# A third PSUM bank in two stages, other gather paces, and part of a one-hot build moved from VectorE to ScalarE

## The chip, the core and the metric

The kernel runs on one core of a Trainium2 chip. A core has five engines with a queue each, and each works through its queue in order: PE (TensorE, the matrix products; PEld is its load of the stationary operand), DVE (VectorE), ACT (ScalarE), POOL (GpSimd, which issues the gathers here) and SP (SyncE, which issues most transfers). They meet through semaphores. Products land in PSUM, eight banks of 128 x 512 f32 numbers; another engine has to carry them out before a bank can be used again. The metric is the device time of one launch in microseconds (us).

## What is computed

One layer of a hybrid trunk over 1024 tokens of width 1024. An attention branch (MLA) and a gated linear attention branch (GLA) are mixed into h; then comes the part on which this change bears, a product-key mixture of 16384 experts, of which each of 8 heads picks 16 per token:

```python
def peer_ffn(h, w_q, sub_keys, u_tab, v_tab):
    q = (h @ w_q).reshape(B, L, PEER_HEADS, 2, PEER_HALF)
    s = jnp.einsum('blhpd,pnd->blhpn', q, sub_keys).astype(jnp.float32)
    top_s, top_i = lax.top_k(s, PEER_TOPK)
    ...
    idx = jnp.take_along_axis(cand_i..., best_pos, axis=-1)   # i * 128 + j
    gate = jax.nn.softmax(best_s, axis=-1)
    ...
        u = u_tab[ib]
        act = jax.nn.gelu(jnp.einsum('bpd,bphkd->bphk', hb, u).astype(jnp.float32), approximate=False)
        coef = (act * gb).astype(hb.dtype)
        return jnp.einsum('bphk,bphkd->bpd', coef, v_tab[ib])
```

## The kernel before

The 1024 tokens are eight blocks of 128, in two groups of four. Each group goes through `mla`, `mix` (GLA and the branch gates), `out_proj`, `norm_ffn` and `route` (the picks). The experts are then computed in two ways at once.

**Gathered.** For blocks 0 to 2 each picked row of u and v is fetched by an indirect transfer on POOL (`gather`, L115), and VectorE takes a dot product with it (L1361) or adds it, scaled, to `acc` (L1377): 448 dots (64 of them for the second half of block 3's tokens, whose results go into the gate values) and 384 adds. They come from one generator, `gather_all`; each call of `weights` takes `self.rate` steps of it. The rates are the constants R_... at the top, and R_VONLY and R_DENSE hold in the dense stage. At most six gathered rows are in flight.

**Dense.** For blocks 4 to 7 and half of block 3 (`DB`, 640 columns, of which 576 take part in the u products) all 16384 experts are computed. The experts are 128 groups `e` of 128: `u_stage(e)` multiplies one 128 x 1024 slice of u with the tokens (48 products of 128 x 288 in two halves, each in a PSUM bank with the tag `tr`) and ScalarE carries each half out with Gelu (L1466). `v_stage(q, half)` multiplies the coefficients of four groups with a half of v's columns (60 products of 128 x 512 in the five banks `mm`), and VectorE adds the five banks to `acc` (L1530). All products are in three parts (L86, L87, L88), since each f32 operand is split into a high part (ScalarE, L79) and a low part (VectorE, L80). So each weight slice costs a transfer of 512 KB (L908), a cast on ScalarE and a subtraction on VectorE. Tags hold two buffers in `tr` and `wr`/`wh`/`wl`, six in `at` and `cf`.

Between them stands the gate: `gate_matrix` turns the picks of the five blocks into a full table of gates per token and expert. Per block, the picks' i, j and gate values are transposed into `tt`. Then 16 rounds follow, each for eight tokens: `gh` holds for each token the 128 x 128 rows (iota == j) * gate (eight instructions, L1619), `oh` the rows (iota == i) for all eight (L1620), TensorE multiplies the two per token (eight products, 16 records, L1625), and ScalarE copies the result from two `mm` banks into `stage` (L1626), which is stored to DRAM (`d_gate`) after every fourth round. `oh` and `gh` are two buffers of the tag `cf`, so three rounds have buffers. 31 of the u stages are woven into these rounds (`weave`), five more must follow the last round (`NLATE`, a dependency on `gm_last`).

In `dense` the gates come back in quarters `q` into `gbuf`; `coef(q, j)` multiplies them with the activations (L1505, the first 576 columns), copies the last 64 columns (L1504) and splits the result into `cf` (L79, L80). Then v stages alternate with the remaining u stages.

The order of the instructions on each engine isn't the order of the code: a scheduler with a timeline of its own fixes it at build time, from the dependencies, the buffers and the code's order as priority. So a change of one buffer count moves instructions in all later stages.

## Time and profile before

| | us |
|---|---|
| three timed runs | 3827.49, 3832.95, 3835.60 (median 3832.95) |
| the profiled execution's own time | 3828.28 |
| its span in the trace | 3826.5 |
| PE busy | 3551.3 (93%) |
| DVE busy | 2999.0 (78%) |
| POOL busy | 1523.7 (40%) |
| ACT busy | 1320.1 (34%) |

The shares are means over stages with different limits. Along the span the stages are: first group up to about 1010 us, attention of the second group to 1250, its mix and projection to 1690, its route to 1950, the gate stage to 2326, v stages alone to about 2750, v and u stages in turn to 3795, and a tail of gathered adds. A matmul's record in the trace is longer than its share of the engine, since matmuls overlap: the distance from start to start tells what one costs. The granted clock (PEclk) is 1.00 at 2.4 GHz and 0.50 at 1.2 GHz.

### The profile page before, as it was taken

The numbers are of one execution on the slowest core, as the hardware profiler recorded it, in microseconds if no ns is written. First come the engines' busy times: TensorE is split into PE (matmuls) and PEld (weight loads), VectorE is DVE, ScalarE is ACT, GpSimd is POOL, SyncE is SP. The second block draws the span as 40 slices with busy tenths as digits, with TensorE's granted clock in tenths as the row PEclk, the third lists the DMA queues.
The fourth block names the chain that finished last, engine by engine and source line by source line (L and its number), as shares of the span: only waits on it lengthen the run. The fifth ranks groups of instructions, "written<-read, shape, count | busy, mean of one in ns | idle before, by whom it ended". The sixth has DMA issues, their size and how long they took to land.

```text
span 3826.5 us, 56688 instructions
## 1 busy us (share of the span) xinstructions
PE 3551.3 (93%) x20380; PEld 3088.1 (81%) x20385; DVE 2999.0 (78%) x6559; ACT 1320.1 (34%) x2851; POOL 1523.7 (40%) x1199
## 2 busy tenths in 40 slices
PE   8899998999799999899999998999999999999996
PEld 8787797777688788679898997777788888888885
DVE  5545444379877667559999997999988988898898
ACT  4656333232366334222244333222222222222221
POOL 2432333334332344322232223444455555555555
PEclk9999999999899999899999999999999999999998
DMA  4544634665324998665567879999999889999888
GB/s 160 173 159 141 222 131 130 192 212 186 124 69 114 341 353 299 268 225 203 171 227 275 288 280 372 332 342 344 332 334 338 303 315 325 322 348 322 298 324 318
DMA packets 390779, 976.98 MB, mean 255 GB/s; under 512 B 40464, under 2 KB 155664, under 8 KB 387680
## 3 DMA queue, kind: packets, MB, share of 16 engines
q1 hardware_dynamic: 242048, 508.50, 37.8%
q0 software_dynamic: 148448, 464.86, 34.6%
q8 instruction: 160, 2.62, 0.3%
q14 instruction: 123, 1.01, 0.1%
HBM read 825.61 MB, written 147.51 MB: 254 GB/s over the span
## 4 chain that ended last, share of the span: by engine, by line
PE 31%; DVE 24%; DMA 9%; issue 5%; ACT 1%; SPq 0%; POOL 0%; ACTq 0%; DVEq 0%; POOLq 0%
PE mm L86 6%; PE mm L87 6%; PE mm L88 6%; DVE cf L1619 4%; DVE acc L1377 3%; DVE row L1361 3%; DVE wl L80 3%; PE tr L88 3%; PE tr L86 3%; DMA wr<-in_uT 3%; PE tr L87 3%; DVE cf L1620 2%; DVE big L1530 2%; DMA row<-in_u,ids 2%; DMA row<-in_v,ids 1%
## 5 line engine op out<-in xcount | busy, mean ns | idle before, releaser
L115 POOL DMA_INDIRECT row<-in_v,ids x384 | 494.6, 1288 | 692.3 <-DVE acc L1377 274.1
L115 POOL DMA_INDIRECT row<-in_u,ids x384 | 479.5, 1249 | 590.8 <-issue 129.9
L86 PE MATMUL tr<-ar,wh 128*128 128x288 f32 x2048 | 616.9, 302 | 32.0 <-ACT at L1466 32.0
L79 ACT CAST wh<-wr 128x1024 fp32r<-128x1024 f32 x344 | 360.4, 1048 | 747.9 <-PE mm L88 302.8
L87 PE MATMUL tr<-ar,wh 128*128 128x288 f32 x2048 | 610.8, 299 | 0.0
L88 PE MATMUL tr<-ar,wl 128*128 128x288 f32 x2048 | 602.7, 301 | 8.5 <-DVE wl L80 8.1
L1361 DVE CUSTOM_DVE_ANT_0 row<-row,n2b 128x1024 f32<-128x1024 f32 x448 | 544.1, 1221 | 60.8 <-DMA row<-in_u,ids 51.0
L87 PE MATMUL mm<-wl,cf 128*128 128x512 f32 x1280 | 508.9, 398 | 5.1 <-DVE wl L80 5.0
L1377 DVE SCALAR_TENSOR_TENSOR acc<-row,act,acc 128x1024 f32<-128x1024 f32 x384 | 491.9, 1281 | 22.2 <-DMA row<-in_v,ids 20.0
L88 PE MATMUL mm<-wh,cf 128*128 128x512 f32 x1280 | 507.8, 397 | 0.0
L86 PE MATMUL mm<-wh,cf 128*128 128x512 f32 x1280 | 443.8, 398 | 15.0 <-DVE big L1530 8.6
L86 PEld LDWEIGHTS tr<-ar,wh 128*128 128x128 f32 x2048 | 392.4, 192 | 38.8 <-ACT at L1466 36.6
L80 DVE TENSOR_TENSOR wl<-wr,wh 128x1024 fp32r<-128x1024 f32 x264 | 324.6, 1229 | 103.2 <-ACT wh L79 98.9
L88 PEld LDWEIGHTS tr<-ar,wl 128*128 128x128 f32 x2048 | 387.5, 191 | 11.7 <-DVE wl L80 11.7
L87 PEld LDWEIGHTS tr<-ar,wh 128*128 128x128 f32 x2048 | 392.3, 192 | 2.1
L80 POOL TENSOR_TENSOR wl<-wr,wh 128x1024 fp32r<-128x1024 f32 x80 | 194.4, 2433 | 326.2 <-ACT wh L79 307.2
L86 PEld LDWEIGHTS mm<-wh,cf 128*128 128x128 f32 x1280 | 238.1, 188 | 80.5 <-ACT wh L79 9.9
L87 PEld LDWEIGHTS mm<-wl,cf 128*128 128x128 f32 x1280 | 241.9, 189 | 65.7 <-DVE wl L80 8.2
L88 PEld LDWEIGHTS mm<-wh,cf 128*128 128x128 f32 x1280 | 242.0, 189 | 58.8
L1530 DVE TENSOR_TENSOR big<-mm,big 128x512 f32<-128x512 f32 x320 | 204.4, 680 | 19.0 <-PE mm L88 18.9
L1466 ACT ACTIVATE at<-tr 128x288 f32<-128x288 f32 x212 | 87.0, 410 | 345.9 <-PE tr L88 326.1
L1625 PE MATMUL mm<-cf,cf 128*128 128x128 f32 x1280 | 158.4, 277 | 28.5 <-DVE cf L1620 28.5
(448 smaller groups left out, 7747.6 us busy)
## 6 DMA issues: line engine op xcount, KB each, us to landing
wr<-in_uT SPq DMA_DIRECT2D x128, 512.0 KB
wr<-in_vb SPq DMA_DIRECT2D x128, 512.0 KB
d_gate<-big SPq DMA_DIRECT2D x20, 2048.0 KB
big<-d_gate SPq DMA_DIRECT2D x128, 320.0 KB
d_wl<-wl SPq DMA_DIRECT2D x72, 512.0 KB
wl<-d_wl SPq DMA_DIRECT2D x72, 512.0 KB
at<-d_act SPq DMA_DIRECT2D x58, 288.0 KB
wr<-in_w_q SPq DMA_DIRECT2D x32, 512.0 KB
```

What stands on the lines that cost most here:

```text
L79: self.pace = self.nc.scalar.copy(hi, src)
L80: i = (eng or self.nc.vector).tensor_tensor(lo, src, hi.bitcast(F32), ALU.subtract)
L86: first = mm(ps, lh, rh, start=start, stop=False)
L87: mm(ps, lh, rl, start=False, stop=False)
L88: self.pe_last = mm(ps, ll, rh, start=False, stop=stop)
L115: i = self.nc.gpsimd.indirect_dma_start(out=out, out_offset=None, in_=self.a[table], in_offset=bass.IndirectOffsetOnAxis(ap=idx, axis=0))
L1361: lag(nc.vector.tensor_tensor_reduce(out=u, in0=u, in1=held[b][0], op0=ALU.mult, op1=ALU.add, scale=1.0, scalar=0.0, accum_out=act[:, 0, k ...
L1377: lag(nc.vector.scalar_tensor_tensor(acc, v, act[:, 1, k:k + 1], acc, ALU.mult, ALU.add))
L1466: self.nc.scalar.activation(at[:, ts], ps[:, :HD], AF.Gelu)
L1530: nc.vector.tensor_tensor(o, ps[b], o, ALU.add)
L1619: nc.vector.tensor_scalar(gh[:, k], self.iota, tt[:, 1, t + k:t + k + 1], tt[:, 2, t + k:t + k + 1], ALU.is_equal, ALU.mult)
L1625: self.gm_last = nc.tensor.matmul(ps[:, k], oh[:, kk], gh[:, kk], start=True, stop=True)
```

## The change

- `gpsum` (mix, route) and `dpsum` (gate stage, dense stage) give tiles without a count of their own three PSUM banks instead of two; with the five `mm` banks that makes eight. The tag `tr` is the one concerned; the three places that name its count say 3.
- R_VONLY goes from 2.5 to 2.6 and R_DENSE from 3.3 to 3.5.
- In `coef` the copy L1504 of the first quarter's coefficients (q = 0, four of 128) is VectorE's.
- In `gate_matrix`, for blocks 4 to 7 and every fourth round, ScalarE builds `gh`: Abs(iota - j), then Relu(gate - 2 * that), which is the gate where j matches and 0 elsewhere, since the gates of these blocks lie between 0 and 1. The negated j is made once per block (`nj`). That is 16 of the 80 rounds; the fifth block, number 3, is built as before.

```diff
@@ -58,7 +58,7 @@
 BANKS = [dict(zip(("S", "tr", "mm", "pv"), map(int, str(x)))) for x in (BA, BB)]
 NGA, NGR, F_MLA = 14, 14, 0.9
 RA0, NRU, NLATE = 7, 22, 5
-R_MLA, R_MIX, R_ROUTE, R_BUILD, R_VONLY, R_DENSE = 0.0, 2.8, 0.7, 2.4, 2.5, 3.3
+R_MLA, R_MIX, R_ROUTE, R_BUILD, R_VONLY, R_DENSE = 0.0, 2.8, 0.7, 2.4, 2.6, 3.5
 
 
 class Layer:
@@ -801,7 +801,7 @@
     def mix_pools(self, ctx):
         if self.grp == 0:
             self.g1 = self.pool(ctx, "yA")
-        self.psum = self.pool(ctx, "gpsum", 2, space=PSUM)
+        self.psum = self.pool(ctx, "gpsum", 3, space=PSUM)
         self.wk = self.pool(ctx, "gw", 2)
         if self.grp == 0:
             self.arp = self.pool(ctx, "arpA", 2)
@@ -959,7 +959,7 @@
             self.weave(self.gla_proj(g, h, st[h], nxt), inner, 1.8)
             self.run(inner)
             inner = self.gla_inner(g, h, st[h])
-        self.weave(self.raw_gates(g, range(first, 2 * NC), ("w_ob", 0), "tr", 2), inner, 1.0)
+        self.weave(self.raw_gates(g, range(first, 2 * NC), ("w_ob", 0), "tr", 3), inner, 1.0)
         self.run(inner)
         if g == 0 and NGF:
             self.fetch_n(self.nh, self.nl)
@@ -1466,7 +1466,7 @@
             self.nc.scalar.activation(at[:, ts], ps[:, :HD], AF.Gelu)
 
     def lead_gate(self, key, nxt):
-        self.run(self.raw_gate(1, self.gate_keys().index(key), nxt, "tr", 2))
+        self.run(self.raw_gate(1, self.gate_keys().index(key), nxt, "tr", 3))
 
     def lead_u(self, key, nxt):
         e = key[1]
@@ -1479,7 +1479,7 @@
     def dense(self, ctx):
 
         nc, a = self.nc, self.a
-        self.psum = self.pool(ctx, "dpsum", 2, space=PSUM)
+        self.psum = self.pool(ctx, "dpsum", 3, space=PSUM)
         self.wk = self.pool(ctx, "dw", 2)
         ng = NK // EG
         ndb = len(DB)
@@ -1501,7 +1501,7 @@
             at = acts.pop(q * EG + j)
             at3 = at.rearrange("p (b t) -> p b t", t=32)
             m = NU // 32
-            nc.scalar.copy(at3[:, m:], gbuf[:, q % 2, m:, j])
+            (nc.scalar.copy if q else nc.vector.tensor_copy)(at3[:, m:], gbuf[:, q % 2, m:, j])
             nc.vector.tensor_tensor(at3[:, :m], at3[:, :m], gbuf[:, q % 2, :m, j], ALU.mult)
             self.split(cf[:, 0], cf[:, 1], at)
 
@@ -1607,6 +1607,9 @@
             nc.tensor.transpose(pt[:, 2], pk["gate"].rearrange("p h k -> p (h k)"), self.ident)
             tt = self.t(self.wk, [P, ND], F32, "at", NAT)[:, 0:3 * P].rearrange("p (a t) -> p a t", a=3)
             nc.scalar.copy(tt, pt[:, 0:3])
+            if blk >= GB:
+                nj = self.t(self.sm, [P, P], F32, "nj128", 2)
+                nc.scalar.mul(nj, pt[:, 1], -1.0)
             yield
             for t32 in range(4):
                 if t32:
@@ -1615,7 +1618,14 @@
                     oh, gh = [self.t(self.wk, [P, 2 * ND], F32, "cf", NCF)[:, 0:NK * G8].rearrange("p (t j) -> p t j", j=NK) for _ in range(2)]
                     t = t32 * 32 + q * G8
                     tb = lambda i: tt[:, i, t:t + G8, None].broadcast_to([P, G8, NK])
-                    for k in range(G8):
+                    if blk >= GB and q == 3:
+
+                        for k in range(G8):
+                            nc.scalar.activation(gh[:, k], self.iota, AF.Abs, bias=nj[:, t + k:t + k + 1])
+                        for k in range(G8):
+                            nc.scalar.activation(gh[:, k], gh[:, k], AF.Relu, bias=tt[:, 2, t + k:t + k + 1], scale=-2.0)
+                    else:
+                      for k in range(G8):
                         nc.vector.tensor_scalar(gh[:, k], self.iota, tt[:, 1, t + k:t + k + 1], tt[:, 2, t + k:t + k + 1], ALU.is_equal, ALU.mult)
                     nc.vector.tensor_tensor(oh, iota, tb(0), ALU.is_equal)
                     for k4 in range(2):
```

The lines of `gate_matrix` move down by ten: L1619 is L1629 after the change, L1620 L1630, L1625 L1635 and L1626 L1636; the new ones are L1624 (Abs) and L1626 (Relu).

**PE at the end of the gate stage.** `tr` is a half of a u stage, `mm` a half round of the gate (two rows of x4 make a round). Before:

```order
L87 MATMUL tr_23306<-ar_16385,wh_23139 128x288
L88 MATMUL tr_23306<-ar_16384,wl_23140 128x288
L1625 MATMUL mm_23222<-cf_23212,cf_23211 128x128 x4
L1625 MATMUL mm_23228<-cf_23212,cf_23211 128x128 x4
L1625 MATMUL mm_23245<-cf_23235,cf_23234 128x128 x4
L1625 MATMUL mm_23251<-cf_23235,cf_23234 128x128 x4
L86 MATMUL tr_23356<-ar_16384,wh_23267 128x288
L87 MATMUL tr_23356<-ar_16385,wh_23267 128x288
```

After (20 rows of L1635 stand here one behind the other; ten are shown):

```order
L87 MATMUL tr_23442<-ar_16385,wh_23275 128x288
L88 MATMUL tr_23442<-ar_16384,wl_23276 128x288
L1635 MATMUL mm_22966<-cf_22956,cf_22955 128x128 x4
L1635 MATMUL mm_22972<-cf_22956,cf_22955 128x128 x4
L1635 MATMUL mm_22989<-cf_22979,cf_22978 128x128 x4
L1635 MATMUL mm_22995<-cf_22979,cf_22978 128x128 x4
L1635 MATMUL mm_23014<-cf_23004,cf_23003 128x128 x4
L1635 MATMUL mm_23089<-cf_23004,cf_23003 128x128 x4
L1635 MATMUL mm_23106<-cf_23096,cf_23095 128x128 x4
L1635 MATMUL mm_23112<-cf_23096,cf_23095 128x128 x4
L1635 MATMUL mm_23129<-cf_23119,cf_23118 128x128 x4
L1635 MATMUL mm_23135<-cf_23119,cf_23118 128x128 x4
```

Before, the u products reach to the last two rounds; after, all of those that may stand ahead of the last round do so ten rounds earlier, and the last ten rounds stand without any between them.

**ACT in a gate round.** After the change, in the first block, from the first copies on (`cf` is `gh`, `big` is `stage`, `at` with `tr` an evacuation of a u stage, `wh` the cast of a weight):

```order
L1636 COPY big_19326<-mm_19346 128x128x4
L1636 COPY big_19326<-mm_19352 128x128x4
L1624 ACTIVATE cf_19471<-iota,nj_3360_19333 128x128 x8
L1466 ACTIVATE at_19663<-tr_19679 128x288
L1626 ACTIVATE cf_19471<-cf_19471,at_19331 128x128 x4
L1636 COPY big_19326<-mm_19369 128x128x4
L1626 ACTIVATE cf_19471<-cf_19471,at_19331 128x128 x3
L1636 COPY big_19326<-mm_19375 128x128x4
L1626 ACTIVATE cf_19471<-cf_19471,at_19331 128x128
L1636 COPY big_19326<-mm_19392 128x128x4
L1636 COPY big_19326<-mm_19464 128x128x4
L79 CAST wh_19806<-wr_19804 128x1024
```

Eight Abs of a later round stand in one piece; the eight Relu are broken up by copies and an evacuation of a u stage, and the next weight's cast stands behind all of them.

**ACT between the gate stage and the first v stage.** `cf` from `at` is the cast of a coefficient, which waits for the gates. Before:

```order
L1466 ACTIVATE at_23495<-tr_23511 128x288
L1466 ACTIVATE at_23495<-tr_23537 128x288
L79 CAST wh_23574<-wr_23572 128x1024
L1504 COPY at_23333<-big_23259 128x64
L1504 COPY at_23409<-big_23259 128x64
L1504 COPY at_23488<-big_23259 128x64
L1504 COPY at_23564<-big_23259 128x64
L79 CAST cf_23335<-at_23333 128x640
L79 CAST cf_23411<-at_23409 128x640
L1466 ACTIVATE at_23571<-tr_23587 128x288
L79 CAST cf_23490<-at_23488 128x640
L1466 ACTIVATE at_23571<-tr_23613 128x288
```

After:

```order
L79 CAST wh_23713<-wr_23711 128x1024
L1466 ACTIVATE at_23631<-tr_23676 128x288
L79 CAST cf_23471<-at_23469 128x640
L79 CAST cf_23550<-at_23548 128x640
L79 CAST cf_23626<-at_23624 128x640
L1466 ACTIVATE at_23710<-tr_23726 128x288
L1466 ACTIVATE at_23710<-tr_23752 128x288
L1466 ACTIVATE at_23779<-tr_23800 128x288
L1504 COPY at_23853<-big_23395 128x64
L1504 COPY at_23855<-big_23395 128x64
L1466 ACTIVATE at_23779<-tr_23826 128x288
L79 CAST wh_23782<-wr_23780 128x1024
```

The four copies have left the queue, and three casts stand where the copies stood, ahead of the same four evacuations (two u stages).

## Rows read from the trace of the kernel before

**Rows 1.** Stretches: us, busy of PE, PEld, DVE, ACT, POOL, clock, DMA share, GB/s

```profile
1950.00:2326.00 376.00, 347.46 (x2761) 341.51 (x2761) 375.97 (x865) 147.70 (x259) 83.98 (x74) 1.00 0.78 278
2420.00:2750.00 330.00, 319.69 (x1349) 251.27 (x1348) 315.48 (x418) 85.11 (x135) 143.36 (x113) 1.00 0.95 340
2750.00:3795.00 1045.00, 1013.14 (x5698) 896.81 (x5696) 925.19 (x1182) 264.84 (x445) 588.49 (x453) 0.99 0.91 322
2361.50:2367.50 6.00, 5.94 (x25) 5.94 (x26) 2.02 (x2) 0.94 (x3) 0.94 (x1) 0.50 1.05 406
```

**Rows 2.** Groups from 1950 to 2326 us: busy, mean ns | idle before

```profile
L1619 DVE TENSOR_SCALAR cf<-iota,at 128x128 f32<-128x128 f32 x640 | 174.7, 352 | 0.0
L1625 PE MATMUL mm<-cf,cf 128*128 128x128 f32 x1280 | 158.4, 277 | 28.5 <-DVE cf L1620 28.5
...
L1377 DVE SCALAR_TENSOR_TENSOR acc<-row,act,acc 128x1024 f32<-128x1024 f32 x35 | 44.8, 1279 | 0.0
...
L80 DVE TENSOR_TENSOR wl<-wr,wh 128x1024 fp32r<-128x1024 f32 x30 | 36.5, 1217 | 0.0
```

**Rows 3.** VectorE in the gate stage in order of time: start, duration

```profile
2100.68 2.14 DVE L1619 TENSOR_SCALAR cf<-iota,at 128x128 f32<-128x128 f32 x8
2102.73 1.22 DVE L1620 TENSOR_TENSOR cf<-iota,at 128x1024 f32<-128x1024 f32 x1
2103.86 1.22 DVE L80 TENSOR_TENSOR wl<-wr,wh 128x1024 fp32r<-128x1024 f32 x1
2105.00 1.22 DVE L1361 CUSTOM_DVE_ANT_0 row<-row,n2b 128x1024 f32<-128x1024 f32 x1
2106.14 0.08 DVE L1361 DVE_READ_ACCUMULATOR2_ANT act<- 128x1 f32 x1
```

**Rows 4.** TensorE: two rows in order of time, then line L1625 (first, last start)

```profile
2104.09 2.02 PE L1625 MATMUL mm<-cf,cf 128*128 128x128 f32 x16 [0.61 <-DVE cf L1620]
2105.87 0.38 PE L88 MATMUL tr<-ar,wl 128*128 128x288 f32 x1
...
L1625 PE MATMUL mm<-cf,cf x1280: 270/275/377, 1955.8 to 2324.9; 128*128 128x128 f32 x183
```

**Rows 5.** TensorE around its stop, in order of time

```profile
2349.03 0.29 PE L86 MATMUL tr<-ar,wh 128*128 128x288 f32 x1
...
2350.49 0.29 PE L88 MATMUL tr<-ar,wl 128*128 128x288 f32 x1
2361.56 0.61 PE L86 MATMUL tr<-ar,wh 128*128 128x288 f32 x1 [10.78 <-ACT at L1466]
```

**Rows 6.** ScalarE groups of near shapes, whole span

```profile
L714 ACT ACTIVATE kjk<-qr 128x128 bf16<-128x128 f32 x64 | 19.8, 309 | 1.1
...
L785 ACT ACTIVATE pr<-S,snm 128x144 f32<-128x144 f32 x16 | 6.1, 383 | 2.8 <-DVE snm L783 2.8
```

**Rows 7.** ScalarE behind the gate stage, in order of time

```profile
2355.47 0.68 ACT L1504 COPY at<-big 128x64 f32<-128x64 f32 x4 [7.38 <-DMA big<-d_gate]
2356.31 1.39 ACT L79 CAST cf<-at 128x640 fp32r<-128x640 f32 x2 [0.16 <-ACT at L1504]
2361.10 0.41 ACT L1466 ACTIVATE at<-tr 128x288 f32<-128x288 f32 x1 [3.40 <-DMA d_act<-at]
2361.41 0.72 ACT L79 CAST cf<-at 128x640 fp32r<-128x640 f32 x1
```

**Rows 8.** VectorE in the tail: first and last row of the 17 adds

```profile
3794.54 5.23 DVE L1377 SCALAR_TENSOR_TENSOR acc<-row,act,acc 128x1024 f32<-128x1024 f32 x4
...
3819.56 2.61 DVE L1377 SCALAR_TENSOR_TENSOR acc<-row,act,acc 128x1024 f32<-128x1024 f32 x2 [0.68 <-DMA row<-in_v,ids]
```

**Rows 9.** TensorE's waits from 2420 to 3795 us: total, times, longest

```profile
PE tr L86 <- ACT at L1466: 21.2, 19, 3.8
```

**Rows 10.** ScalarE, then TensorE, around 2965 us, in order of time

```profile
2964.56 1.04 ACT L79 CAST wh<-wr 128x1024 fp32r<-128x1024 f32 x1 [14.47 <-DMA wr<-in_uT]
...
2965.97 0.61 PE L86 MATMUL tr<-ar,wh 128*128 128x288 f32 x1 [3.59 <-ACT at L1466]
```

## The prediction

> **What bounds the kernel now.** I read the stretches first, since the page's shares average over stages with different limits [rows 1]. In the gate stage (1950 to 2326 us) VectorE is busy 375.97 of 376 us, TensorE 347, ScalarE 148: VectorE is the bound there, and nowhere later so clearly. From 2420 to 2750 us (v stages alone) TensorE has 320 of 330 and VectorE 315: nearly level. From 2750 to 3795 us TensorE has 1013 of 1045 and VectorE 925: TensorE is the bound, beside DMA engines at 0.91. So a cut in VectorE's work is worth most in the gate stage, little in the next, nothing in the long last one. Then I read who waits in the gate stage [rows 2]: TensorE's one-hot matmuls (L1625) wait 28.5 us in all for VectorE, and the VectorE groups have no idle time before them.
>
> **The gate stage.** VectorE's prices are taken from start to start [rows 3]: eight gated rows of L1619 take 2102.73 - 2100.68 = 2.05 us (0.256 each), the one-hot of i (L1620) 1.13, a weight's low half (L80) 1.14, a dot product of a gathered row (L1361) 1.14. Busy means are 0.08 longer, as the 1.22 of L80 against 1.14; a gathered add (L1377) with a mean of 1.279 [rows 2] is then 1.20. The order before has, between the first and the last of the 80 rounds, 640 rows of L1619, 80 of L1620, 29 of L80, 35 dots and 35 adds: 163.8 + 90.4 + 33.1 + 39.9 + 42.0 = 369 us. That is the stage, so the prices hold. After, 16 rounds (every fourth of four of the five blocks) leave their 128 gated rows to ScalarE: minus 128 x 0.256 = 32.8 us. The order adds one L80 and two dots and drops an add in the stretch: 339 us. If VectorE stayed the bound all through, the stage would lose **30 us**.
>
> It doesn't stay so. On TensorE a round is 16 records, of which the next work starts 2105.87 - 2104.09 = 1.78 us later [rows 4], and a record of a u product (128x288) is (2350.49 - 2349.03) / 11 = 0.133 us [rows 5]. Before: 80 x 1.78 + 1427 x 0.133 = 332 us, well under VectorE's 369. After, 1173 u products stand ahead of the first round instead of 1117 (7 us more, of which some 2 fall into holes), and the order has moved u products ahead in the stage too: by round 65 TensorE has 65 x 1.78 + 1253 x 0.133 = 282 us to do, VectorE up to round 67, the most that six cf buffers (three rounds) let it be ahead, 408 x 0.256 + 67 x 1.13 + 58 x 1.14 + 28 x 1.20 = 280 us. So TensorE, now without its 28.5 us of waits, sets the pace up to there. Then the u products run out (the last ten rounds stand in one piece) and VectorE has 13 rounds left, all in the old form, the fifth block's: 104 x 0.256 + 13 x 1.13 + 9 x 1.14 + 6 x 1.20 = 59 us, which nothing covers. From first to last round: 5 + 282 + 59 = 346 against 369 (1955.8, the first round, to 2324.9 [rows 4]). That is 23; for late gated rows I take off 3: **-20 us**, with 10 and 30 as ends.
>
> ScalarE's side has no row of this form. Below is L714 with 0.309 us for 128x128 without a pointer operand, above L785, 0.383 for 128x144 out of PSUM with one [rows 6]. Successors overlap by some 0.05 to 0.1, as L79's 1.39 for two casts where one takes 0.72 [rows 7]. I take 0.30 per activation, nearer the upper row since both passes have a pointer as bias: 256 x 0.30 = 77 us on an engine with 376 - 148 = 228 free. No table load was added among them. ScalarE therefore has the time; what it can lose is the order, below.
>
> The Trainium skill (ScalarE: Activation LUTs, Rules for kernel authors) says to put relu and the like on VectorE and not on ScalarE, which speaks against this change. By its formula in the section on ACT_TABLE_LOAD (pointer bias 280 ns + 0.833 ns per element, less 93 of overlap) two passes cost an estimated 0.59 us for VectorE's 0.256, and counted as engine time the edit would lose 256 x 0.294 - 33 = 42 us. The stretch contradicts the use of that rule here, as VectorE is full and ScalarE 39% busy; no run here shows Abs or Relu yet.
>
> **From the last round to the first v product.** TensorE stops for 10.78 us at 2350.49 [rows 5]. ScalarE's queue explains it [rows 7]: the copies of L1504 wait for the gates to come back from DRAM until 2355.47, then casts, and the next evacuation (L1466) waits 3.40 us more for a d_act store that had to free its buffer. The two tr banks are full meanwhile. After it the granted clock is 0.50, the 1.2 GHz level [rows 1]: 25 records in 6 us, 0.24 apart instead of 0.133; over the 24 to 48 records of the spell that costs some 3 us. The q = 0 copies now go to VectorE, but the order shows that ScalarE gains nothing directly: three casts of cf, which need the same gates through VectorE, take the place of the copies ahead of the last four evacuations. What helps is the third tr bank: half a u product more (24 x 0.133 = 3.2 us) before the stop, and less clock lost. Against that TensorE comes out of ten thin rounds (1.78 us of work in some 4.5) and may start its u products at 1.2 GHz. Ends: 0 and 14; I take **-7 us**.
>
> **The pace.** R_VONLY from 2.5 to 2.6: in the 24 steps from the first to the twenty-fifth v stage the order has 130 gathered dots and adds instead of 124, 6 x 1.17 = 7 us of VectorE where it is nearly level with TensorE (15 us free [rows 1]). **+4 us**, ends 0 and 7. R_DENSE from 3.3 to 3.5: in the order each v stage with two u products holds 12 gathered operations before and after; something else holds the gathers there, so nothing changes. What comes of both is the tail: 17 adds stand behind the last L1530 before, 12 after. From 3794.54 to 3822.17 the 17 took 27.6 us, 1.63 each, a part of it waiting for rows [rows 8]; five fewer: **-8 us**, ends -5 and -10.
>
> **The third tr bank elsewhere.** From 2420 us TensorE waits 21.2 us in 19 pieces for ScalarE's evacuation [rows 9], so a third bank looks worth those 21 us and the clock lost after them. One level up it isn't so: at 2961 to 2966 ScalarE's weight cast (L79) had waited 14.47 us for the transfer from in_uT and ended at 2965.60; the evacuation behind it in the queue let TensorE go at 2965.97 [rows 10]. The next u product needs that very weight, so a free bank would have gained 0.37 us. I count 0, with -15 as end. In the mix stages no wait of the trace names a tr bank: 0, with 8 either way for the new order.
>
> **Sum.** -20 - 7 + 4 - 8 = -31 us. On the profiled execution's own 3828.28 that gives 3797; its span is 3826.5. The median of the three runs, 3832.95, is 4.7 higher and gives 3802. I take **3799 us**.
>
> **The rivals.** (1) VectorE stays the bound to the end, because TensorE finds holes for the moved u products: 30 instead of 20 in the stage, and the freed bank gives a little more: 3775 to 3787. For it: VectorE has no idle time at all in the stage. Against: the 59 us at its end. Chance 0.17. (2) ScalarE is late. In its queue the casts of weights and evacuations stand behind eight Abs or Relu; VectorE's L80 waits for the casts, TensorE for the rest. Half the stage's gain goes: 3812 to 3825. Against: three of five banks and buffers as cover. Chance 0.16. (3) The same mechanism beyond its cover makes it **slower**. A gated round's row buffer comes free three rounds ahead, 3 x 4.2 = 12.6 us; sixteen activations (4.8 us at 0.30) and what stands among them (148 / 80 = 1.85 us of other ScalarE work a round [rows 1], over two rounds some 4) take 9. Each us beyond 12.6 stops TensorE 16 times; the chain must reach 15 us, 0.69 us an activation, for the whole 31 and 8 more to go: 3841 to 3860. No row is near that price. Chance 0.07. (4) The change moves nothing that can be told: a new order in the mix stages or a later gate transfer takes the gain: 3825 to 3840. Chance 0.07.
>
> **How the numbers follow.** The forecast, 3787 to 3812, has what is left, 0.53. The range may leave out 0.2: (3), (4) and the upper third of (2): 3776 to 3820. A measurement of this kernel can tell some 0.2% from no change, 7.7 us. Faster by more: forecast, (1) and (2), 0.86; within it 0.07; slower 0.07.
>
> **What would show it.** Right: in the profile after, the last L1625 (now L1635) some 20 us earlier, its waits for VectorE gone from the first four blocks and present in the fifth; VectorE with idle time in the stage; Abs and Relu at 0.35 to 0.42 us each; 12 adds in a tail of some 20 us; the 3 to 4 us stops at weights from in_uT still there. Wrong: TensorE's waits for L1626 (Relu), L80 waiting for ScalarE's casts in the gate stage, or a gate transfer that lands as late as before.

## The result and the profile after the change

The changed kernel takes **3795.97 us** (median of six runs, 3791.68 to 3801.69) beside 3829.69 before (six runs, 3824.69 to 3835.60): ratio **0.9931**, 95% interval 0.9916 to 0.9946. (Ratios and intervals are the recorded ones throughout; the quotient of the two medians alone is 0.9912, so a step of 0.002 between two ratios should not be leaned on.) The profiled run has a span of 3794.4 us, 32.1 less than before. The forecast was 3799 within 3776 to 3820.

Where the 32 us come from is read by cutting both traces at the same instructions. The marks: the first instruction of L1050 (mix of the first group begins), the first of L354 (its end), the first u product, the first and the last one-hot product on TensorE, the first v product, the end of the last L1530 of the 24th v stage (the v stages alone) and of the 64th, the end. Each number is the distance of two marks in one trace, in us.

| kernel | first group's mix, route | first u to first round | first to last round | last round to first v | v stages alone | v and u stages | tail |
|---|---|---|---|---|---|---|---|
| before | 633.0 | 262.3 | 369.1 | 45.9 | 368.0 | 1055.8 | 31.9 |
| after | 621.6 | 273.1 | 347.0 | 38.3 | 376.6 | 1049.4 | 22.9 |
| difference | -11.4 | +10.8 | -22.1 | -7.6 | +8.6 | -6.4 | -9.0 |

The two stretches that are left out (up to L1050, and from L354 to the first u product) differ by +6.5 and -1.4. The second holds the second group's mix and route, where the third bank counts too. No line of the change bears on the first, and in the fourteen traces of this study it lies between 372.9 and 384.8: a single trace tells nothing below some 6 us in it. The v and u stages range from 1041 to 1060.

**The gate stage.** Stretches of the kernel after (columns as in [rows 1]):

```profile
1960.00:2250.00 290.00, 290.00 (x2354) 290.00 (x2353) 279.87 (x588) 193.63 (x478) 92.10 (x62) 1.00 0.84 303
2250.00:2308.00 58.00, 45.02 (x322) 43.39 (x321) 58.00 (x132) 19.41 (x35) 14.60 (x11) 0.88 0.81 290
2380.00:2720.00 340.00, 319.48 (x1331) 249.87 (x1330) 320.55 (x425) 87.61 (x141) 152.70 (x118) 0.99 0.96 341
2734.00:3768.00 1034.00, 1007.86 (x5698) 894.99 (x5697) 919.61 (x1171) 264.16 (x443) 587.14 (x449) 0.99 0.91 324
```

One bound has become two. Up to 2250 us TensorE is busy 290.00 of 290 and VectorE 279.87; from there VectorE has 58.00 of 58 and TensorE 45.02, its granted clock down to 0.88 between the thin rounds. Before, VectorE was full all through [rows 1]. The line of the one-hot products (start of the first and the last; [rows 4] before), the only wait of TensorE's matrix products in these rounds (total, times, longest), and VectorE's one-hot rows of i of rounds 67 and 80:

```profile
L1635 PE MATMUL mm<-cf,cf x1280: 270/275/554, 1960.2 to 2307.2; 128*128 128x128 f32 x183
```

```profile
PE mm L1635 <- DVE cf L1630: 13.0, 8, 3.4
```

```profile
2244.49 1.22 DVE L1630 TENSOR_TENSOR cf<-iota,at 128x1024 f32<-128x1024 f32 x1
...
2303.44 1.21 DVE L1630 TENSOR_TENSOR cf<-iota,at 128x1024 f32<-128x1024 f32 x1
```

The waits for VectorE fell from 28.5 us [rows 2] to 13.0, and all eight lie in the last stretch: none is left before 2250 us. The thirteen rounds behind round 67 take VectorE 2303.44 - 2244.49 = 58.95 us.

What VectorE itself waited for in the stage:

```profile
DVE wl L80 <- ACT wh L79: 7.4, 3, 2.9
DVE cf L1629 <- PE mm L1635: 2.5, 2, 1.7
```

So TensorE's buffers held VectorE for 2.5 us, the last time at 2089 us, and ScalarE's casts of weights held it for 7.4 us, the last time at 2231; before, it sat idle for nothing [rows 2]. At round 67 VectorE starts its gated rows at 2242.41, 3.7 us after round 64's products (2236.80 to 2238.75) had freed the buffers. So up to 3.7 of the 347 us may be casts that came late; no run isolates that.

ScalarE's new instructions (minimum/median/maximum ns), then a gated round of it in order of time:

```profile
L1624 ACT ACTIVATE cf<-iota,nj x128: 386/390/407, 1962.7 to 2229.7; 128x128 f32<-128x128 f32 x128
```

```profile
L1626 ACT ACTIVATE cf<-cf,at x128: 385/392/414, 1965.3 to 2233.3; 128x128 f32<-128x128 f32 x128
```

```profile
2047.63 2.45 ACT L1624 ACTIVATE cf<-iota,nj 128x128 f32<-128x128 f32 x8
2049.99 2.14 ACT L1626 ACTIVATE cf<-cf,at 128x128 f32<-128x128 f32 x7
```

Eight Abs hold the engine (2049.99 - 2047.63) = 2.36 us, 0.295 each, and none of TensorE's waits names a Relu.

**Behind the gate stage.** TensorE at the end of its u products, then the cast on ScalarE that it waits for ([rows 5, 7] before):

```profile
2339.18 0.29 PE L88 MATMUL tr<-ar,wl 128*128 128x288 f32 x1
2345.50 2.50 PE L86 MATMUL mm<-wh,cf 128*128 128x512 f32 x5 [6.03 <-ACT wh L79]
```

```profile
2344.40 1.04 ACT L79 CAST wh<-wr 128x1024 fp32r<-128x1024 f32 x1 [4.04 <-DMA wr<-in_vb]
```

The stop of 10.78 us for an evacuation is gone: the 240 late u products run from 2307.23 to 2339.18 without a hole. What is left are 6 us for v's first weight, which comes late (the DMA engines' share from 2310 to 2345 us is 1.04). The gates, too, are back sooner: their first use (L1504, 2326.35) starts 19.2 us behind the last one-hot product, before 30.5 [rows 4, 7].

**The tail**, VectorE in order of time ([rows 8] before):

```profile
3770.82 0.68 DVE L1530 TENSOR_TENSOR big<-mm,big 128x512 f32<-128x512 f32 x1
3771.42 6.56 DVE L1377 SCALAR_TENSOR_TENSOR acc<-row,act,acc 128x1024 f32<-128x1024 f32 x5
3779.55 1.28 DVE L1377 SCALAR_TENSOR_TENSOR acc<-row,act,acc 128x1024 f32<-128x1024 f32 x1 [1.58 <-DMA row<-in_v,ids]
3782.01 7.89 DVE L1377 SCALAR_TENSOR_TENSOR acc<-row,act,acc 128x1024 f32<-128x1024 f32 x6 [1.17 <-DMA row<-in_v,ids]
```

Twelve adds in 3789.90 - 3771.42 = 18.5 us, where 17 took 27.6.

### The profile page after: what moved, and what is told of

It is laid out like the page before. It is cut to its first block, busy times and chain, and to the rows that moved or that the text cites. A ratio compares the mean times of both kernels' runs of the same rounds, so it can differ in the third digit from the quotient of the medians.

```text
span 3794.4 us, 56822 instructions
## 1 busy us (share of the span) xinstructions
PE 3544.1 (93%) x20385; PEld 3088.2 (81%) x20385; DVE 2962.8 (78%) x6435; ACT 1390.0 (37%) x3109; POOL 1551.9 (41%) x1199
## 3 DMA queue, kind: packets, MB, share of 16 engines
q1 hardware_dynamic: 242048, 508.50, 38.3%
## 4 chain that ended last, share of the span: by engine, by line
PE 37%; DVE 18%; DMA 9%; issue 4%; ACT 2%; POOL 0%; SPq 0%; DVEq 0%; ACTq 0%; POOLq 0%
PE mm L86 6%; PE mm L87 6%; PE mm L88 6%; PE tr L88 4%; PE tr L86 4%; PE tr L87 4%; PE mm L1635 3%; DMA wr<-in_uT 3%; DVE acc L1377 3%; DVE row L1361 3%; DVE wl L80 2%; DVE big L1530 2%; DMA row<-in_u,ids 1%; DMA row<-in_v,ids 1%; DMA wr<-in_vb 1%
## 5 line engine op out<-in xcount | busy, mean ns | idle before, releaser
L115 POOL DMA_INDIRECT row<-in_v,ids x384 | 505.2, 1316 | 703.8 <-DVE acc L1377 232.6
L115 POOL DMA_INDIRECT row<-in_u,ids x384 | 496.4, 1293 | 504.9 <-ACT wh L79 153.2
L86 PE MATMUL tr<-ar,wh 128*128 128x288 f32 x2048 | 610.6, 300 | 15.4 <-ACT wh L79 13.8
L80 DVE TENSOR_TENSOR wl<-wr,wh 128x1024 fp32r<-128x1024 f32 x264 | 323.6, 1226 | 113.3 <-ACT wh L79 109.6
L86 PEld LDWEIGHTS tr<-ar,wh 128*128 128x128 f32 x2048 | 389.2, 190 | 19.3 <-ACT wh L79 15.4
L80 POOL TENSOR_TENSOR wl<-wr,wh 128x1024 fp32r<-128x1024 f32 x80 | 195.6, 2448 | 329.1 <-ACT wh L79 319.6
L1530 DVE TENSOR_TENSOR big<-mm,big 128x512 f32<-128x512 f32 x320 | 204.3, 679 | 18.4 <-PE mm L88 18.2
L1466 ACT ACTIVATE at<-tr 128x288 f32<-128x288 f32 x212 | 86.4, 409 | 287.6 <-PE tr L88 286.5
L79 ACT CAST cf<-at 128x640 fp32r<-128x640 f32 x128 | 92.8, 728 | 263.3 <-PE mm L88 251.7
```

The source lines that it names most:

```text
L79: self.pace = self.nc.scalar.copy(hi, src)
L80: i = (eng or self.nc.vector).tensor_tensor(lo, src, hi.bitcast(F32), ALU.subtract)
L86: first = mm(ps, lh, rh, start=start, stop=False)
L115: i = self.nc.gpsimd.indirect_dma_start(out=out, out_offset=None, in_=self.a[table], in_offset=bass.IndirectOffsetOnAxis(ap=idx, axis=0))
L1466: self.nc.scalar.activation(at[:, ts], ps[:, :HD], AF.Gelu)
L1530: nc.vector.tensor_tensor(o, ps[b], o, ALU.add)
```

## Experiments: each part alone

Four kernels each carry one part of the change, one carries all but the gate edit. Edits, as parts of the diff shown above: gate edit alone (`gate_only`), `dpsum` 2 to 3 alone (`dbank_only`), `gpsum` 2 to 3 with the two named counts alone (`gbank_only`), the two paces alone (`paces_only`).

```diff
-        self.psum = self.pool(ctx, "dpsum", 2, space=PSUM)
+        self.psum = self.pool(ctx, "dpsum", 3, space=PSUM)
```

**The gate edit alone.** 

> The kernel before with the gate edit alone (Abs and Relu in every fourth round of blocks 4 to 7), its two-bank pools, paces and copies kept. In its order 1115 u products stand ahead of the first round (before 1117, after 1173) and they last to round 77 of 80 (after: 70). Theory A (VectorE and TensorE race each other, as in the prediction): TensorE has work to round 77, so VectorE with its 336 to 339 us stays the bound to the end and the fifth block's 59 us are covered: first to last round 338 to 343 us instead of 369, nothing else moves, 26 to 31 us faster than before, ratio 0.992 to 0.9935: as fast as the whole change without any of its other parts. Theory B (the stage's gain needs the third bank, without which TensorE stops at evacuations that stand behind eight activations on ScalarE): 350 to 360 us for the stage, 8 to 18 us faster, ratio 0.995 to 0.998, with waits of TensorE for L1466 in the stage.

**The dense bank alone.** 

> The kernel before with three instead of two banks in the dense pool alone. 1174 u products stand ahead of the first gate round instead of 1117. Theory A (the bank moves work but VectorE remains the bound of the gate stage; the stops at L1466 from 2420 us on are late weights): the first round 4 to 7 us later, still 367 to 371 us to the last, the stop behind the stage 3 to 7 us shorter, the 21 us of waits for L1466 from 2420 us on still 15 or more, 18 instead of 17 adds in the tail: within 5 us of before, ratio 0.999 to 1.0015. Theory B (the waits for evacuation were a lack of banks): these waits under 8 us, 10 to 20 us faster, ratio 0.995 to 0.9975.

**The paces alone.** 

> The kernel before with R_VONLY 2.6 and R_DENSE 3.5 alone. In the order 130 instead of 124 gathered operations stand between the first and the twenty-fifth v stage, 13 instead of 17 adds behind the last L1530. Theory A (the prediction's terms): the stretch with v stages alone 0 to 7 us longer, the tail 4 x 1.6 = 6 us shorter: between 7 us faster and 2 us slower, ratio 0.998 to 1.0005. Theory B (VectorE has room in the first stretch, so that the pace is free): stretch unchanged, 6 to 8 us faster, ratio 0.998. Theory C (VectorE holds TensorE there): the stretch 7 us or more longer, no gain at all, ratio 1.000 to 1.001.

**Everything but the gate edit.** 

> The changed kernel without its gate edit (all one-hot rows on VectorE as before), with the third banks, the paces and the copy on VectorE. Theory A: first to last round 367 to 371 us as before, first round 4 us later, transition 5 us and tail 8 to 9 us shorter: 6 to 13 us faster than before, ratio 0.9965 to 0.9985, so that the gate edit is 20 to 27 of the whole 34 us. Theory B (the third bank and the pace carry the gain): 20 us or more faster, ratio under 0.995.

**The mix bank alone** (made later, when the traces had shown the first stages shorter). 

> The kernel before with the third bank in the mix and route pool alone. Six traces with that bank reach the first u product at 1680 to 1690 us, four without it at 1694 to 1698. Theory A (the bank is worth something in the first group's mix, which the prediction took as 0 with 8 either way): that mark 8 to 14 us earlier than in before, 5 to 14 us faster in all, ratio 0.9965 to 0.9985. Theory B (the spread of the first stages from run to run, or one of the other edits, made that difference): within 4 us of before, ratio 0.999 to 1.001.

| kernel | ratio to before, 95% | mix, route | u to round | rounds | to v | v alone | v and u | tail |
|---|---|---|---|---|---|---|---|---|
| gate edit alone | 0.9937 (0.9914 to 0.9959) | 638.8 | 262.3 | 341.6 | 48.7 | 369.5 | 1049.3 | 31.3 |
| dense bank alone | 1.0002 (0.9989 to 1.0016) | 631.8 | 268.6 | 369.8 | 41.2 | 370.1 | 1047.9 | 30.4 |
| mix bank alone | 0.9958 (0.9939 to 0.9977) | 621.1 | 264.0 | 368.7 | 45.3 | 368.3 | 1054.2 | 32.0 |
| paces alone | 0.9982 (0.9968 to 0.9996) | 633.5 | 262.4 | 369.0 | 45.6 | 369.8 | 1055.6 | 24.6 |
| all but the gate edit | 0.9996 (0.9979 to 1.0012) | 625.3 | 273.0 | 369.9 | 40.8 | 381.3 | 1052.6 | 22.2 |

*Gate edit.* Theory A: 341.6 us for the rounds (338 to 343 were expected), u products up to round 77, so most of the fifth block's rounds are covered. First and last start of its one-hot products, then the stretch:

```profile
L1635 PE MATMUL mm<-cf,cf x1280: 270/275/377, 1960.3 to 2301.9; 128*128 128x128 f32 x183
```

```profile
1960.00:2302.00 342.00, 336.41 (x2722) 335.05 (x2722) 337.14 (x722) 214.30 (x514) 109.66 (x71) 1.00 0.82 301
```

TensorE 336 and VectorE 337 of 342 us: this is the race, nearly even to the end. No third bank is needed for it. By the ratios the gate edit alone (0.9937) can't be told from the whole change (0.9931).

*Dense bank.* Theory A's time: no gain. It pulls 57 u products ahead of the first round (+6.3) and takes 4.7 from the way to v. But it isn't theory A's trace: no wait for the evacuation L1466 is left behind 2380 us, where 15 us or more were expected. What came in its place? TensorE's waits in the v and u stages (total, times, longest), with the dense bank alone, then in the changed kernel:

```profile
PE tr L86 <- ACT wh L79: 19.3, 7, 4.5
```

```profile
PE tr L86 <- ACT wh L79: 13.8, 7, 2.9
```

The 21.2 us that stood against L1466 [rows 9] have changed their name: with the bank alone TensorE stops for nearly the same time (19.3) at the weight itself, in the changed kernel for 13.8. There, ScalarE's cast and TensorE's next product:

```profile
2947.03 1.04 ACT L79 CAST wh<-wr 128x1024 fp32r<-128x1024 f32 x1 [7.14 <-DMA wr<-in_uT]
```

```profile
2948.13 0.61 PE L86 MATMUL tr<-ar,wh 128*128 128x288 f32 x1 [2.50 <-ACT wh L79]
```

*Mix bank.* 0.9958, more than theory A's 0.9965 to 0.9985, and a first group that is 12 us shorter. But the mark that theory A named, the first u product, comes only 3.9 us earlier (1689.6 beside 1693.5; 8 to 14 were expected): between L354 and it, in the second group, 7.5 us are lost again in this trace, whose execution (3823.89 us) is 5.6 above the median of its nine. All ten traces with this bank have 618.4 to 626.2 us there, all four without it 631.8 to 638.8. TensorE, PEld, VectorE and the rest from 620 to 1000 us, before and with the mix bank alone:

```profile
620.00:1000.00 380.00, 343.50 (x1641) 278.27 (x1642) 268.38 (x1134) 110.72 (x177) 140.59 (x83) 0.97 0.57 185
```

```profile
620.00:1000.00 380.00, 350.35 (x1643) 283.81 (x1644) 270.08 (x1146) 118.85 (x216) 147.25 (x95) 0.96 0.59 192
```

Seven us more of TensorE's work fit into the same 380 us. Which of the re-ordered waits gives them wasn't isolated.

*Paces.* 0.9982; the tail is 7.3 us shorter and the v stages alone are 1.8 longer, inside what theory A gave.

*All but the gate edit.* Neither theory: within 0.2% of nothing, where its parts taken alone (-0.42, +0.02 and -0.18%) promise -0.58%. Its trace says where they went: 7.7 us gained in the mix and 9.7 in the tail, 10.7 lost ahead of the first round and 13.3 in the v stages alone (its profiled execution, 3831.51 us, is 9 above the median of its twelve, so some of that may be this execution's). The second loss has no part that makes it alone (+2.1, +0.3, +1.8). So **the parts don't add up** here. For the whole change it stays open: by the ratios -1.21% as a sum (without the copies, which were not run alone) stands against -0.69% measured, by the quotients of the medians -0.97% against -0.88%.

## Experiments: ScalarE's price, the banks and the copies

**More work in ScalarE's chain**: four more Abs passes between Abs and Relu.

```diff
                             nc.scalar.activation(gh[:, k], self.iota, AF.Abs, bias=nj[:, t + k:t + k + 1])
+                        for k in range(G8):
+                            nc.scalar.activation(gh[:, k], gh[:, k], AF.Abs)
...
```

> The changed kernel with four more passes of Abs (|x| is its own Abs, so nothing else is altered) between Abs and Relu of each ScalarE round: 48 activations instead of 16, the added 32 at an estimated 0.2 to 0.29 us. A round's chain is then 4.7 + 6.4 to 9.4 + 4 = 15 to 18 us against the 12.6 us that the buffers of three rounds cover, ScalarE's sum 138 + 77 + 102 to 150 = 317 to 365 us. Theory A (the prediction's price of a late ScalarE: each us beyond 12.6 stops TensorE, 16 times): 38 to 90 us slower than the change, 3835 to 3885 us, with TensorE's first product of each such round waiting for Relu. Theory B (only ScalarE's sum counts, since the scheduler starts Abs earlier): stage 347 to 366 us, 0 to 20 us slower than the change.

Ratio 0.9980 (0.9966 to 0.9994), 3817.74 us, some 20 slower than the change: between the theories. The rounds take 374.1 us, 27 more. TensorE's waits in the gate stage (L1643 are its one-hot products, L1634 Relu, L1638 VectorE's rows of i):

```profile
PE mm L1643 <- ACT cf L1634: 18.9, 3, 6.6
PE mm L1643 <- DVE cf L1638: 16.6, 14, 1.4
PE mm L1643 <- ACT cf L1624: 2.9, 2, 1.4
```

The added passes, without a pointer operand, cost 0.200 each, so the chain was 4.7 + 32 x 0.2 + 4 = 15 us. Theory A wanted a stop in each of the sixteen rounds; there are five, 21.8 us in all. The order filled the time with u products and used the last of them ahead of round 55, so that TensorE had nothing but the rounds themselves for the last 26 of them. A late ScalarE does cost: some 20 us, about half of the least (38) that the prediction's price gave.

**Twice as many rounds on ScalarE**, with three and with two dense banks:

```diff
-                    if blk >= GB and q == 3:
+                    if blk >= GB and q % 2 == 1:
```

> The changed kernel with every second round of blocks 4 to 7 on ScalarE (32 rounds instead of 16, 512 activations at 0.293 us = 150 us beside 138 us of other ScalarE work in the stage). VectorE's sum falls by another 33 us to about 306, and u products last to round 78. Theory A (the race of VectorE and TensorE decides, ScalarE has time): TensorE sets the pace all through, 80 x 1.78 + 1371 x 0.133 = 325 us: first to last round 325 to 332 us instead of 347, 10 to 20 us faster than the change, ratio to before 0.988 to 0.991. Theory B (the order of ScalarE's queue decides: at 288 of 330 us it is late for TensorE's banks and for the weights' casts): 340 us or more, no faster than the change, with TensorE waiting for L1636, L1626 or L79.

> As the run with 32 rounds on ScalarE, with two banks again in the dense pool: 1116 u products ahead of the first round, the rest last to round 78. Theory A: TensorE 80 x 1.78 + 1428 x 0.133 = 332 us from the first round, which is 4 to 8 us earlier: the last round at about the time of the run with three banks, the stop behind it 7 to 10 us longer: 5 to 10 us slower than that run, ratio 0.990 to 0.993. Theory B (ScalarE late, and a bank fewer gives it less cover): 345 us or more, slower than the change.

| kernel | ratio to before, 95% | mix, route | u to round | rounds | to v | v alone | v and u | tail |
|---|---|---|---|---|---|---|---|---|
| 32 rounds | 0.9919 (0.9902 to 0.9935) | 618.5 | 274.1 | 333.8 | 50.1 | 376.3 | 1041.5 | 26.2 |
| 32 rounds, two dense banks | 0.9902 (0.9879 to 0.9925) | 622.0 | 264.1 | 337.6 | 46.9 | 369.7 | 1059.5 | 23.4 |
| change, two dense banks | 0.9918 (0.9899 to 0.9938) | 621.5 | 264.1 | 349.1 | 39.7 | 382.1 | 1052.8 | 24.1 |
| change, copies on ScalarE | 0.9938 (0.9915 to 0.9960) | 626.2 | 272.9 | 347.8 | 38.9 | 378.3 | 1055.6 | 22.5 |

With three banks the stretch of the rounds, and the wait of VectorE's gated rows for buffers (total, times, longest):

```profile
1956.00:2290.00 334.00, 328.88 (x2666) 328.50 (x2665) 300.65 (x584) 271.17 (x746) 93.18 (x70) 0.99 0.81 299
```

```profile
DVE cf L1629 <- PE mm L1635: 27.3, 16, 3.0
```

The roles are exchanged: TensorE is the bound (328.88 of 334), VectorE waits for it, and ScalarE with 271 us holds TensorE for only 5.1 us in two pieces (a weight's cast and an evacuation). That is theory A's 325 to 332 but for 2 us. But of the 13 us won in the rounds some 5 are left in the ratios (0.9919 beside 0.9931, which their intervals don't tell apart): the way to the first v product grew from 38.3 to 50.1. ScalarE there:

```profile
2338.92 1.04 ACT L79 CAST wh<-wr 128x1024 fp32r<-128x1024 f32 x1 [7.52 <-DMA wr<-in_vb]
```

Beside the change v's first weight is cast only 5.5 us earlier (2344.40 there), though the last round starts 17.3 us earlier; what held it wasn't tested. With two banks the same edit gave 3783.46 us, not slower as expected: the first round starts 10 us sooner after the first u product, and the ratios don't tell the two apart.

**The change with two dense banks.** 

> The changed kernel with two banks again in the dense pool alone. 1116 u products stand ahead of the first round instead of 1173, and they last to round 74 instead of 70. Theory A (the dense bank gives at the stop behind the stage what it costs at its start and end, net nothing): first to last round 340 to 345 us instead of the 347.3 of the change, the first round 4 to 8 us earlier, the way from the last round to the first v product 45 to 49 us instead of 38, the v stages no longer than in the change: within 5 us of the change, ratio to before 0.9915 to 0.9945. Theory B (the dense bank is part of the gain): 8 us or more slower than the change, ratio above 0.995. Theory C (it is a net cost that the sum of the parts hides: the gate edit alone gave 0.9937 and the paces alone 0.9982): ratio under 0.9915.

Theory A in the total (0.9918 beside 0.9931), though the interval doesn't exclude theory C's 0.9915, and not in its terms: the rounds took 349.1 instead of 340 to 345, the way to v 39.7 instead of 45 to 49, and the v stages alone 382.1, 5.5 longer than in the change.

**The change with the first quarter's copies on ScalarE.** 

> The changed kernel with the first quarter's coefficient copies on ScalarE again. From the last round to the first v product it was 45 to 49 us in three traces without the dense bank and without the copy edit, 38 to 41 in those with the bank, but 39 also in one with the copy edit and no bank. Theory A (the bank alone shortens it, the copies do nothing): 38 to 41 us, the whole within 4 us of the change, ratio to before 0.9925 to 0.9945. Theory B (copies that wait for the gates in ScalarE's queue are what stops TensorE): 45 us or more, 5 to 8 us slower than the change.

38.9 us to the first v: with three dense banks the copies are not what stops TensorE, theory A. With two banks they were not tested by themselves. The median, 3809.53, is higher with its companions of before; its ratio, 0.9938, is that of the change within the intervals.

**Later u stages, and the pace of the v stages alone.** Both on the kernel with 32 rounds and two banks:

```diff
-RA0, NRU, NLATE = 7, 22, 5
+RA0, NRU, NLATE = 7, 22, 6
```

> The kernel with 32 rounds on ScalarE and two dense banks, with NLATE 6 instead of 5: one u stage (48 products, 6.4 us) more is kept for behind the last round. Theory A (TensorE is the bound of the gate stage now, and behind it a fixed way of about 48 us, store and return of the gates, passes before the first v product): first to last round 327 to 331 us instead of 337, the stop of 8.8 us behind it down to 2 to 4, the first v product 5 to 7 us earlier: 3776 to 3779 us, ratio 0.988 to 0.990. Theory B (the stop is a place in ScalarE's queue and moves along with the later u stage): last round 6 us earlier, first v product where it was, no gain.

> As the run with NLATE 6, with R_VONLY back at 2.5 (R_DENSE stays 3.5): 124 instead of 129 gathered operations from the first to the twenty-fifth v stage, 15 instead of 13 adds in the tail. Theory A (the pace costs VectorE where it is level with TensorE: 357 against 352 us in the means of seven and three traces): that stretch 3 to 8 us shorter, the tail 3 us longer: 0 to 5 us faster than the run with NLATE 6. Theory B (the difference of the stretches is the spread of runs): the stretch as long, 3 us slower through the tail.

The first: 0.9894 (0.9873 to 0.9916), 3790.30 us. The rounds took 339.8 us, no less than with five: in them TensorE now waits 9.0 us in five pieces for VectorE's rows of i, where it waited 0.8. To the first v it is 48.1, with 288 late u products instead of 240, and the longest stop there shrank from 8.5 to 5.5. Theory B in what it gained: nothing that the ratios show. The second: 0.9936 (0.9912 to 0.9960), against theory A: with *fewer* gathered operations the v stages alone took 381.2 us instead of 375.4.

Of the three kernels with 32 rounds and two dense banks two are ahead of the change (0.9902 and 0.9894 beside 0.9931), the third, with the old pace of the v stages alone, is not (0.9936). The intervals touch or overlap, so that they beat the kernel before is shown, that the two beat the change only likely.

## Why the prediction was right, step by step

- **The race in the gate stage: right in place, and in size but for its seams.** 282 us to round 65 were forecast, 282.5 measured (1960.2 to 2242.7, its start); 59 for the thirteen rounds at the end, 58.95 measured. The sum was 346 from first to last round with 5 for the late start in it, so 341 without; 347.0 were measured without it. The 6 us are what the sum had nothing for: 1.8 from the start of round 65 to VectorE's rows of i of round 67 (2242.71 to 2244.49), and 3.8 from those of round 80 to the last product (2303.44 to 2307.20). VectorE's 339 us also hold: 2304.65 - 1953.89 = 350.8 from its first gated row, less the 10.1 that it sat idle. The edit alone and its doubled form confirm the mechanism from both sides: where u products last, VectorE's sum is the stage (341.6); where VectorE has less to do than TensorE, TensorE's sum is (333.8).
- **Mis-sized inside that step:** the stretch ahead of the first round, into which 56 u products moved, grew by 10.8 us, not 5. The dense bank alone, with 57 moved, has +6.3, the mix bank alone, with none moved, +1.7; the rest has no run of its own. With that the stage's net is -22.1 + 10.8 = -11.3 instead of -20. The last product still starts 17.7 us earlier (2324.9 to 2307.2), since the mix gave 11.4 us that were not in the sum, less 6.5 from a longer stretch ahead of it.
- **ScalarE's price: right.** 0.293 in the median from start to start, estimated 0.30; 75 us of ScalarE bought 33 of VectorE and some 24 of the whole (gate edit alone). By the figures of the Trainium skill (ScalarE: Activation LUTs, What ACT_TABLE_LOAD costs) an estimate is 280 + 0.833 x 128 - 93 = 294 ns with a pointer operand and, with immediates, 186 + 107 - 93 = 200; the runs show 293 and 200 (the added Abs passes). The Trainium skill's rule against relu on ScalarE (same page, Rules for kernel authors) goes by the time per element; the gate edit alone was faster against it, 0.9937.
- **The way to the first v: right in size (-7.6 for -7), half right in its reason.** The dense bank is what changes it (-4.7 alone), as forecast, but it removed the whole stop for an evacuation, not the 3.2 us of it that were reckoned, and a late weight took part of that back. The two-bank kernel with 39.7 shows that another order does the same.
- **The v stages alone: the term that left its ends (0 to 7).** +4 was forecast for six more gathered operations, +8.6 came. With the pace alone it is +1.8, inside the ends, and 381.2 us with the old pace in the last run. So the pace was priced about right, and something that the sum had at nothing came on top. It is idle time of TensorE: that grew from 14.7 to 22.3 us in the stretch, and without it the stretch is 353 us before and 354 after, 352 to 357 in all fourteen traces. Its largest part is TensorE's wait for VectorE's emptying of the five banks (total, times, longest), from the first to the 24th v stage, before, after, and all but the gate edit:

```profile
PE mm L86 <- DVE big L1530: 8.6, 14, 1.5
```

```profile
PE mm L86 <- DVE big L1530: 12.8, 11, 2.8
```

```profile
PE mm L86 <- DVE big L1530: 15.3, 16, 3.0
```

  So in part it would be where L1530 stands among VectorE's gathered operations, which each order sets anew; that is read off, not tested. And it isn't always this wait: the run with four Abs passes has 7.0 there and 10.4 for casts of weights, with 377.2 us. Why eight of the nine kernels that combine parts take 375 us and more here, the six other kernels 370 and less, stays open.
- **The tail: right.** Twelve adds, -9.0 for a forecast -8.
- **The third dense bank in the v and u stages: right within the noise.** The ratio with it alone is 1.0002, the stops have another name. The 6.4 us less in that stretch lie inside its spread.
- **The mix: mis-sized.** 0 with 8 either way was taken because no wait named a bank of this tag. The bank gives 12 us in the first group (11.9 with it alone, 11.4 in the change). As far as direct waits go the argument was sound; a new order it had at 8 either way, and the first group gained more than that. That the new order fills idle time of TensorE is read from the two rows above; what the second group does with the bank differs from trace to trace (L354 to the first u product 680.8 to 689.7 us with it, 681.1 to 682.4 without).
- **The sum** of -31 came out as -32 partly by compensation: -11.3 for the stage (forecast -20), -7.6 for the way to v (-7), +8.6 for the v stages alone (+4), -9.0 for the tail (-8), then -11.4 in the mix and -6.4 in the v and u stages (0 and 0), +6.5 ahead of the mix, where no line of the change bears, and -1.4 in the second group. The race and the tail were understood, the way to v in part; that the total fell within 3 us of the forecast is luck.
- **The rivals.** VectorE as the bound to the end is what the edit does alone, not in the change. A late ScalarE doesn't stop TensorE in the change: none of TensorE's waits names Relu. But one of the signs that the prediction listed as wrong is there: L80 waits for ScalarE's casts in the gate stage, the 7.4 us above, which may have cost up to 3.7. The sum had 3 us for late gated rows; the rows were not late, the casts were.

## What to carry to other kernels

Price a move between engines as a race: add up each engine's work to the point where one runs out of filler, and only then ask who ends last; here that gave 282 + 59 us before the run. A wait's name is the last releaser: before adding a buffer for it, look one level up, since of the 21 us of "evacuation" 19 came back with the bank alone under the name of the weight. Where a scheduler fixes the order, test parts in combination, since here everything but the gate edit gave -0.04% where its parts promise -0.58%.

## What was not expected of the hardware

The same code ahead of the first mix took 372.9 to 384.8 us in fourteen traces, so a single trace can't settle a few us there. And ScalarE at 271 of 334 us busy, in an order of eight passes at a time, kept TensorE waiting for only 5.1 us and VectorE for 4.1: the doubled rounds show no wait of TensorE's products for L1626 in the stage, and for L1636 none with three dense banks and 1.5 us with two.
